# A scratch tile of 64 bytes a partition instead of 32, in front of the last SBUF pool

## The chip, the cores and the metric

The kernel runs on one core of one Trainium2 chip. The core has a matmul engine (TensorE, PE in the profile; its weight loads have a row of their own, PEld), a vector engine (VectorE, DVE), a scalar engine (ScalarE, ACT), GpSimd (POOL), and a queue engine (SyncE, SP) that here does nothing but issue transfers. Operands lie in SBUF, a memory of 128 partitions; an address here means the byte offset within a partition. Matmul results go to PSUM. The metric is device time in microseconds (us) of one execution. All sizes of SBUF tiles below are bytes a partition.

## The reference: what is computed

One encoder layer over 1024 positions of 1024 channels, in float32. A vector `c` gives six modulation rows through `silu(c) @ w_ada + b_ada`: shift, scale and gate (`gt1`, `gt2`) of two sub-layers.

```python
h = rmsnorm(x, norm1_g) * (1.0 + sc1) + sh1
u, v, q, k, va, gate_a, gate_b = split(h @ w_in)
a_out = gmlp_branch(u, v, ...) @ w_a
b_out = window_attention_branch(q, k, va, ...) @ w_b
merged = sigmoid(gate_a) * a_out + sigmoid(gate_b) * b_out
x = x + gt1 * (merged @ w_o)
h2 = rmsnorm(x, norm2_g) * (1.0 + sc2) + sh2
f_gate, f_up = split(h2 @ w_ffn_in)
x = x + gt2 * ((silu(f_gate) * f_up) @ w_ffn_out)
```

The attention looks at most 128 positions away and has 8 heads of 64; the feed-forward part (FFN) is 2816 wide.

## The kernel before, in words

**Split matmuls.** Each float32 operand is stored as a high part in the matmul's own number format (`fp32r`) and a low part that holds the rest. A product of two blocks is then three matmuls: high by high, high by low, low by high. ScalarE writes the high parts (`A.copy`), VectorE subtracts for the low parts. In the profile a matmul line names its PSUM bank first (`mm` or `at`) and then the two operands, in alphabetical order: `at<-tt1h,wh` has the weights `wh` as the stationary operand and the token tile `tt1h` as the moving one. All the big matmuls are 128 rows by 128 columns of weights against 512 moving columns.

**Stages.** `half(0)` and `half(1)` compute the normalised input, the input projections, the gMLP branch, the attention and the branch projections for the two halves of the positions. `gate_products` computes the sigmoid gates and the merge for six of the eight channel blocks, `out_products` the projection with `w_o` and the sums for the second norm. Then come the first and the second FFN matrix. From `gate_products` on, each 2 by 2 block product is done with seven block products instead of eight: sums of blocks are formed on VectorE first. The seven steps are listed in `STEPS` (line 1374), and each is 12 matmuls (`multiply`, line 1378). In their order, the moving operand is `B11`, `B21`, `T2`, `T1`, `T3`, `B22`, `T4`. `gate_products` runs the seven steps 6 times, the first FFN matrix 22 times (of its first six units the first two steps are done ahead), and `out_products` has them 4 times in another order.

**Where the moving operands lie.** `B11` and `B21` lie in `hpool` (tiles `h`), `T3` and `T4` in `mid`. `T1`, `T2` and `B22` lie in the pool `ffn` (tiles `tt1h`, `tt1l`, `tt2h`, `tt2l`, `b22h`, `b22l`, made by `fpt`, line 1248). The weights come from `wpool` (`wh`, `wl`), with one exception: the weights `first`, of two units, lie in `ffn`. In the second FFN matrix (`step_mm`) both operands of a step lie in one tile: 512 weight columns and 512 token columns side by side, for three steps of five in `wpool` (`wh`, `wl`), for the other two in the pool `outp` (`oh`, `ol`).

**The pools.** SBUF pools are laid one behind another in the order in which they are opened, and the tiles in a pool likewise; each tile's size is rounded up to a multiple of 32 bytes. The order is `const`, `wpool` (9 tiles of 4096), `hpool` (4 of 8192), `mid` (8 of 8192), `t2` (8 of 2048), `small`, and behind `small` one pool after another at the same place: `apool` with `attp` behind it during the two halves, then `ffn` from `open_ffn` on (line 573), then `outp` (line 2126). The tiles of `small`, rounded, with their numbers:

| tile of `small` | bytes, number | sum |
|---|---|---|
| `es`, `ms`, `qms`, `qrs`, `nmx`, `den`, `vr`, `ngt` | 32, 4 of each | 1024 |
| `ss` | 2560, 1 | 2560 |
| `kms`, `krs` | 64, 4 of each | 512 |
| `ngt1` | 32, 1 | 32 |
| all | | 4128 |

`wpool`, `hpool`, `mid` and `t2` are together 151552 bytes, a multiple of 2048. So the last pool begins 151552 + 4128 = 155680 bytes behind the start of `wpool`, and 155680 = 64 x 2432 + 32. The tiles of `ffn` and `outp` are all 4096 or 8192 bytes, and every matmul operand begins at a multiple of 512 within its tile. So an operand in `ffn` or `outp` and an operand in `wpool`, `hpool` or `mid` lie a multiple of 64 plus 32 bytes apart, and two operands of `wpool`, `hpool` and `mid` a multiple of 512 apart, as are two operands that both lie in `ffn` or `outp`. In `apool` the key tile `kbuf` too lies a multiple of 64 plus 32 bytes from `wpool`, and so do the tiles of `attp` (`pH`, `pL`, `vt`).

**The order of the work.** In `half` and `gate_products` the instructions of each engine run in the order of the program. In `out_products` a small planner (`Plan`) orders them by written costs; it knows nothing of addresses. The FFN's order is written out by hand (`tc.manual_schedule`).

Of the kernel before, what the change touches and what calls it, by code (L numbers as in the profile page):

```python
# [8 lines left out]
F32 = mybir.dt.float32  # L9
# [3 lines left out]
ALU = mybir.AluOpType  # L13
# [3 lines left out]
P = 128  # L17
D = 1024
S = 1024
KT = D // P  # L20
# [87 lines left out]
def kernel(  # L108
# [43 lines left out]
    V, A, G, T = (Engine(e) for e in (nc.vector, nc.scalar, nc.gpsimd, nc.tensor))  # L152
# [8 lines left out]
    small = ctx.enter_context(pool("small", 4))  # L161
# [21 lines left out]
    def midt(dt, shape):  # L183
        return mid.tile([P, 2048], dt, tag="mid", name=nm("mid")).rearrange(
            "p (a b) -> p a b", a=shape
        )
# [6 lines left out]
    def sm(n, name):  # L193
        return small.tile([P, n], F32, tag=name, name=nm(name))
# [76 lines left out]
    mod = const.tile([P, 48], F32, tag="mod", name="mod")  # L271
    acc_mod = const.tile([P, 48], F32, tag="acc_mod", name="acc_mod")
    SH1, SC1, GT1, SH2, SC2, GT2 = (8 * i for i in range(6))
# [1217 lines left out]
    def out_products(merged):  # L1491
# [5 lines left out]
        B22 = oblk["B22"] = (fpt("b22h"), fpt("b22l"))  # L1497
        T3 = oblk["T3"] = (midt(F32R, 4), midt(F32R, 4))
        T4 = oblk["T4"] = (midt(F32R, 4), midt(F32R, 4))
        ngt = small.tile([P, KT], F32, tag="ngt1", name="ngt1", bufs=1)  # L1500
        V.tensor_scalar(ngt, mod[:, GT1 : GT1 + KT], -1.0, None, op0=ALU.mult)
        gt = mod[:, GT1 : GT1 + KT]

        def negsum(out, a, b):
# [279 lines left out]
    with tc.manual_schedule():  # L1784
        out_products(merged)
# [263 lines left out]
    with tc.manual_schedule():  # L2049
# [141 lines left out]
        ngt = sm(4, "ngt")  # L2191
# [130 lines left out]
```

## Time and profile before

| what | us |
|---|---|
| median of 3 runs | 1232.06 |
| lowest, highest of the runs | 1232.01, 1233.99 |
| the profiled execution's own time | 1234.32 |
| its span, first to last instruction | 1232.5 |
| PE busy in the span | 1220.7 |
| DVE busy | 928.6 |
| ACT busy | 582.6 |
| granted TensorE clock, mean | 0.999 |

The profile is of one execution. Its span is the time from the first to the last instruction on the chip; the execution's own time stands 1.8 us above it. Matmuls overlap: one that is shown with 390 ns may begin 227 ns after the one before. What a matmul costs in a row of them is therefore the distance between starts. The chain view gives that: it follows the work that ended last back from the end and merges pieces of one kind, so that a piece `x12` of 2.72 us is twelve matmuls, one every 227 ns.

### The profile page before, as it was taken

To read this page: it belongs to the slowest core of one execution; us is meant where nothing else is said; L and a number is where in the kernel's file an instruction comes from. 1 tells how busy PE (TensorE), PEld (TensorE's weight loads), DVE (VectorE), ACT (ScalarE), POOL (GpSimd) and SP (SyncE) were. 2 spreads that over 40 slices of the span, in tenths; PEclk is the share of its full clock that TensorE was granted. 3 is DMA by queue.
4 is the path that set the end of the run, shared out by engine and by line. 5 is a ranking of instruction groups with operands and counts; after the bars stand their busy time and mean duration, and the time that the engine had idled before them with its cause. 6 is when DMAs were issued, how large, how long until landed. Compare 5 with 4: busy or idle time off the path is not lost.

```text
span 1232.5 us, 15626 instructions
## 1 busy us (share of the span) xinstructions
PE 1220.7 (99%) x5653; PEld 1006.7 (82%) x5653; DVE 928.6 (75%) x1504; ACT 582.6 (47%) x954; POOL 150.6 (12%) x182
## 2 busy tenths in 40 slices
PE   8999999999999999999999999999999999999998
PEld 7888888888788888878778888888888888888887
DVE  8999977789978766898897667575676766665646
ACT  5667855367855443645453333333333334433341
POOL 0024323114322000011000000000000000010001
PEclk9999999999999999999999999999999999999999
DMA  9752169654276333476403446454555439995552
GB/s 363 275 185 96 35 228 362 230 188 154 103 258 237 110 113 104 147 232 227 137 35 120 171 158 218 177 187 182 188 188 188 169 147 366 394 357 188 188 171 103
DMA packets 78096, 236.54 MB, mean 192 GB/s; under 512 B 8898, under 2 KB 9154, under 8 KB 72772
## 3 DMA queue, kind: packets, MB, share of 16 engines
q1 hardware_dynamic: 63028, 163.20, 38.4%
q0 software_dynamic: 14992, 72.36, 15.6%
q8 instruction: 44, 0.72, 0.2%
q14 instruction: 32, 0.26, 0.1%
HBM read 176.28 MB, written 59.24 MB: 191 GB/s over the span
## 4 chain that ended last, share of the span: by engine, by line
PE 91%; DVE 4%; DMA 2%; ACT 2%; issue 1%; SPq 0%; ACTq 0%; DVEq 0%
PE mm L145 46%; PE at L145 45%; DVE mid L145 2%; DMA raw<-in_w_q_dram 1%; DMA ws<-in_w_up_dram 1%; DVE wl L145 0%; ACT lb L145 0%; DMA mid<-in_xA_dram 0%; ACT mid L145 0%; DVE lb L145 0%; ACT pH L145 0%; DVE wo L145 0%; DVE ss L145 0%; DVE pL L145 0%; DVE xs L145 0%
## 5 line engine op out<-in xcount | busy, mean ns | idle before, releaser
L145 DVE TENSOR_TENSOR wl<-raw,wh 128x1024 fp32r<-128x1024 f32 (+1 forms) x135 | 158.8, 1180 | 61.7 <-ACT wh L145 61.2
L145 ACT CAST wh<-raw 128x1024 fp32r<-128x1024 f32 (+1 forms) x149 | 152.0, 1022 | 110.9 <-PE mm L145 36.4
L145 PE MATMUL mm<-mid,wh 128*128 128x512 f32 x640 | 198.7, 391 | 0.7 <-DVE mid L145 0.7
L145 PEld LDWEIGHTS mm<-mid,wh 128*128 128x128 f32 x640 | 119.8, 188 | 26.8 <-DVE mid L145 1.1
L145 PE MATMUL mm<-wh,h 128*128 128x512 f32 x384 | 124.6, 396 | 1.6 <-ACT h L145 1.6
L145 PE MATMUL mm<-mid,wl 128*128 128x512 f32 x320 | 124.9, 390 | 0.0
L145 PE MATMUL at<-h,wh 128*128 128x512 f32 x304 | 94.1, 391 | 1.3 <-DVE t L145 1.3
L145 PE MATMUL mm<-h,wh 128*128 128x512 f32 x304 | 94.3, 391 | 0.0
L145 PEld LDWEIGHTS mm<-wh,h 128*128 128x128 f32 x384 | 70.8, 188 | 15.2 <-ACT h L145 1.9
L145 DVE TENSOR_TENSOR wl<-ws,wh 128x1024 fp32r<-128x1024 f32 (+1 forms) x54 | 60.7, 1124 | 25.0 <-ACT wh L145 25.0
L145 ACT CAST wh<-ws 128x1024 fp32r<-128x1024 f32 (+1 forms) x54 | 52.6, 973 | 43.8 <-DVE ws L145 31.5
L145 PE MATMUL mm<-wl,h 128*128 128x512 f32 x192 | 71.2, 391 | 0.0
L145 PEld LDWEIGHTS mm<-mid,wl 128*128 128x128 f32 x320 | 60.0, 188 | 13.6
L145 PEld LDWEIGHTS at<-h,wh 128*128 128x128 f32 x304 | 56.8, 188 | 13.7 <-DVE t L145 2.1
L145 PEld LDWEIGHTS mm<-h,wh 128*128 128x128 f32 x304 | 56.6, 188 | 11.7
L145 ACT ACTIVATE t<-t 128x512 f32<-128x512 f32 x46 | 28.4, 630 | 71.7 <-DVE t L145 71.6
L145 DVE TENSOR_TENSOR ol<-raw,oh 128x1024 fp32r<-128x1024 f32 x30 | 36.6, 1223 | 31.4 <-ACT oh L145 29.8
L145 PE MATMUL mm<-h,wl 128*128 128x512 f32 x152 | 59.3, 390 | 0.0
L145 PE MATMUL at<-h,wl 128*128 128x512 f32 x152 | 59.2, 389 | 0.0
L145 ACT ACTIVATE xs<-xs 128x512 f32<-128x512 f32 x21 | 13.3, 632 | 96.2 <-DVE xs L145 96.2
L145 PE MATMUL at<-wl,wh 128*128 128x512 f32 (+1 forms) x136 | 52.8, 389 | 0.0
L145 PE MATMUL at<-wh 128*128 128x512 f32 (+1 forms) x136 | 52.8, 388 | 0.0
(296 smaller groups left out, 2866.0 us busy)
## 6 DMA issues: line engine op xcount, KB each, us to landing
mid<-in_w_ada_dram SPq DMA_DIRECT2D x28, 512.0 KB, 8.8
raw<-in_w_gate_dram SPq DMA_DIRECT2D x28, 512.0 KB, 3.8
tA<-hid POOLq DMA_DIRECT2D x11, 1024.0 KB, 4.4
tB<-hid POOLq DMA_DIRECT2D x11, 1024.0 KB, 5.0
wo<-in_w_out_dram POOLq DMA_DIRECT2D x22, 512.0 KB, 6.1
wS<-wo POOLq DMA_DIRECT2D x11, 1024.0 KB, 5.3
raw<-wS SPq DMA_DIRECT2D x44, 256.0 KB, 3.1
raw<-tB SPq DMA_DIRECT2D x44, 256.0 KB, 5.3
```

The lines of the kernel that those rows point to most:

```text
L145: ins = f(*args, **kw)
```

## The change

The tile `ngt1`, which holds the negated gates of the first sub-layer in `out_products`, is made 16 floats wide instead of 8. Only its first 8 columns are written and read. It takes 64 bytes instead of 32 in `small`, so `small` takes 4160 bytes instead of 4128. `ngt`, which stands behind `ngt1`, and everything in the pools behind `small` (`apool`, `attp`, `ffn`, `outp`) begin 32 bytes higher. The distance from `wpool` to the last pool becomes 155712 = 64 x 2433, an odd number of 64s. The pools before `small` stay where they are, and no instruction is added, removed or moved to another engine.

```diff
@@ -1497,8 +1497,8 @@
         B22 = oblk["B22"] = (fpt("b22h"), fpt("b22l"))
         T3 = oblk["T3"] = (midt(F32R, 4), midt(F32R, 4))
         T4 = oblk["T4"] = (midt(F32R, 4), midt(F32R, 4))
-        ngt = small.tile([P, KT], F32, tag="ngt1", name="ngt1", bufs=1)
-        V.tensor_scalar(ngt, mod[:, GT1 : GT1 + KT], -1.0, None, op0=ALU.mult)
+        ngt = small.tile([P, 16], F32, tag="ngt1", name="ngt1", bufs=1)
+        V.tensor_scalar(ngt[:, :KT], mod[:, GT1 : GT1 + KT], -1.0, None, op0=ALU.mult)
         gt = mod[:, GT1 : GT1 + KT]
```

## Prediction

> **What bounds the kernel now.** I read the page first: the busy times, the granted clock, the chain by engine.
>
> ```profile
> span 1232.5 us, 15626 instructions
> PE 1220.7 (99%) x5653; PEld 1006.7 (82%) x5653; DVE 928.6 (75%) x1504; ACT 582.6 (47%) x954; POOL 150.6 (12%) x182
> PEclk9999999999999999999999999999999999999999
> PE 91%; DVE 4%; DMA 2%; ACT 2%; issue 1%; SPq 0%; ACTq 0%; DVEq 0%
> ```
>
> TensorE is busy for 99% of the span at the full granted clock, and the chain that ends last runs through it for 91%. The reader is to see that the matmuls are the bound and that the clock isn't. So the question is whether a matmul itself can be cheaper. The chain view in order of time (start, length, what) shows that equal matmuls do not cost the same. The long run of 204 matmuls is from the end of the second half, the next rows are from the gate products, the others from the FFN:
>
> ```profile
> 346.97 46.28 PE mm L145 x204
> 412.61 2.72 PE at L145 x12
> 415.32 2.80 PE mm L145 x12
> 418.13 2.80 PE at L145 x12
> 420.93 2.76 PE mm L145 x12
> ...
> 763.41 5.48 PE mm L145 x24
> 768.89 2.72 PE at L145 x12
> 771.61 2.80 PE mm L145 x12
> 774.41 2.80 PE at L145 x12
> 777.21 2.76 PE mm L145 x12
> 779.97 2.80 PE at L145 x12
> 782.77 5.48 PE mm L145 x24
> ```
>
> Read from 768.89: the seven steps of one FFN unit, twelve matmuls each, in the order of the code. B21 takes 2.72, T2 2.80, T1 2.80, T3 2.76, B22 2.80, and the last piece of 24 is T4 with the next unit's B11, 5.48. From 763.41 to 782.77 is one period: 19.36 us for 84 matmuls. In the long run of 204 one matmul takes 46.28 / 204 = 226.9 ns, in a step of 2.72 it takes 226.7 ns, in one of 2.80 it takes 233.3 ns. All three steps of 2.80 have their moving operand in the pool `ffn`; no other step has. T3, with its operand in `mid`, follows such a step and takes 2.76.
>
> Who is slow is told by operand in the groups kept apart by form. The means are modelled durations, longer than the distance between starts, but they differ by the same 5 to 6 ns:
>
> ```profile
> L145 PE MATMUL mm<-mid,wh 128*128 128x512 f32 x640 | 198.7, 391 | 0.7 <-DVE mid L145 0.7
> L145 PE MATMUL at<-h,wh 128*128 128x512 f32 x304 | 94.1, 391 | 1.3 <-DVE t L145 1.3
> L145 PE MATMUL at<-tt1h,wh 128*128 128x512 f32 x112 | 44.3, 395 | 0.0
> L145 PE MATMUL at<-tt2h,wh 128*128 128x512 f32 x88 | 34.9, 396 | 0.0
> L145 PE MATMUL mm<-b22h,wh 128*128 128x512 f32 x72 | 28.6, 397 | 0.0
> L145 PE MATMUL at<-oh,ol 128*128 128x512 f32 x84 | 32.9, 391 | 0.0
> L145 PE MATMUL at<-pH,vt 128*128 128x512 f32 x44 | 17.4, 396 | 0.0
> L145 PE MATMUL mm<-h,first 128*128 128x512 f32 x24 | 5.9, 395 | 0.0
> ```
>
> Now put the distances between the two operands beside them, taken to multiples of 64 bytes. `mid` or `h` with `wh`: no remainder, 391. `tt1h`, `tt2h`, `b22h` with `wh`: 32 bytes over, 395 to 397. `first` with `h`: here the weights lie in `ffn` and the moving operand doesn't, 32 over again, 395. `oh` with `ol`: both in the last pool, no remainder between them, 391. So it is not the pool's place that costs, nor an operand that begins off a multiple of 64 by itself. It is a pair whose two operands lie 32 bytes apart in that count. One row speaks against it: `pH` with `vt`, both in `attp`, is slow at 396 without a remainder. Those come in runs of two to six between shapes of another kind, and T3 above shows that a pair without remainder needs a run-in: its first twelve take 2.76 and not 2.72. I take the row for such a run-in.
>
> **The change part by part.** The instruction that writes the wider tile is the same one, over the same 8 columns (172 ns, below), and it stays where the planner put it: 0. Everything behind `small` moves by 32 bytes. What else works on those tiles is not sensitive to the place:
>
> ```profile
> L145 DVE TENSOR_SCALAR ngt<-mod 128x8 f32<-128x8 f32 x1 | 0.2, 172 | 0.0
> L145 DVE TENSOR_TENSOR tt1l<-mid,tt1h 128x512 fp32r<-128x512 f32 x12 | 8.0, 684 | 1.4 <-ACT tt1h L145 1.4
> L145 DVE TENSOR_TENSOR mid<-mid,mid 128x512 fp32r<-128x512 f32 x26 | 16.9, 683 | 0.1
> L145 ACT CAST tt1h<-mid 128x512 fp32r<-128x512 f32 x12 | 7.2, 618 | 6.2 <-DVE mid L145 6.1
> L145 ACT CAST mid<-mid 128x512 fp32r<-128x512 f32 x26 | 14.8, 620 | 6.5 <-DVE mid L145 6.4
> ws<-in_w_up_dram SPq DMA_DIRECT2D x11, 512.0 KB, 5.7
> ru<-in_w_up_dram SPq DMA_DIRECT2D x11, 512.0 KB, 3.6
> ```
>
> VectorE takes 684 ns with `ffn` and 683 without, ScalarE 618 and 620. The same weights land in 3.6 us in `ru`, which is in `ffn`, and in 5.7 us in `ws`, which is in `mid`: 32 bytes cost a transfer nothing that shows. All these terms are 0, covered by a TensorE that is busy 99% in any case.
>
> The matmuls, for pairs that after the change lie an odd number of 64s apart:
> - Steady. Three steps in the `ffn` pool, 12 matmuls each, in 6 + 22 units of the gates and the FFN and 4 of `out_products`: 32 x 36 = 1152 matmuls. 233.3 - 226.7 = 6.6 ns each: 7.6 us.
> - Run-ins. T3 and T4 follow such a step in each of 28 units: 2.76 - 2.72 = 0.04 us, 56 times: 2.2 us. In `out_products` two or three more: 0.1.
> - The 48 matmuls with `first` save 0.3 us by the same price, but they end in the stretch below where VectorE is late: 0. That stretch is what comes next when a matmul gets cheaper: from 593.56 to 621.55 the chain leaves TensorE, waits for a transfer and then goes through VectorE. It starts from sums that follow the matmuls before it, so what is won before it is kept, and what is won inside it is not.
>
> ```profile
> 593.56 6.64 DMA ws<-in_w_up_dram
> 600.22 0.70 DVE ws L145
> 621.55 30.86 PE at L145 x132
> ...
> 1017.85 60.11 PE at L145 x264
> ```
>
> - The second FFN matrix. 60.11 / 264 = 227.7 ns against 226.7: the run-ins between `wh` and `oh`, 1.0 ns x 924 matmuls = 0.9 us. A pair of it that straddles the switch goes from 32 over to none, so it may gain all of it or none; I take 0.4.
> - The attention. `kbuf` comes level with its weights, but in runs of two matmuls, which stay in the run-in: 0, at most 0.5.
>
> Sum: 7.6 + 2.2 + 0.1 + 0.4 = 10.3 us. TensorE must find its operands that much earlier. In the FFN this is no difficulty:
>
> ```profile
> 800.00:900.00 100.00, 100.00 (x436) 81.36 (x435) 67.51 (x94) 33.16 (x46) 7.60 (x15) 1.00 0.50 179
> 900.00:1000.00 100.00, 100.00 (x436) 81.44 (x435) 67.96 (x95) 34.10 (x47) 9.60 (x18) 1.00 0.54 191
> ```
>
> In these rows of 100 us (PE, PEld, DVE, ACT, POOL busy, then clock and DMA share) VectorE has 32 us to spare and the DMA engines half their time; 1.6% more speed leaves that cover standing. I take off 0.3 for waits elsewhere: 10.0 us. Against the profiled span, 1232.5 to 1222.5; its own time of 1234.32 is the launch's 1.8 us more and lies 2.3 above the median shown, which is where the next forecast starts: 1232.06 - 10 = 1222.
>
> The unknown in this: the trace of before has no row of a pair 64 bytes over. All its pairs are a multiple of 512 apart or 32 over. Both ends come from the nearest rows. If 64 over is like none, -10.3. If the cost grows with the distance, 32 bytes are 6.6 ns and 64 are 13.2: the same terms again with the other sign, +10. I take the first, because the rows come back to the same 391 for two quite different no-remainder cases (`mid` with `wh`, and `oh` with `ol`), and a pattern that repeats every 64 bytes is the shortest that fits them.
>
> [...]
>
> **The rivals.**
> - *64 over is a worse phase, not a good one.* The place is the same 1152 matmuls. For it: no pair in the trace has this distance, and a pattern that repeats every 128 bytes fits the rows too. Against it: it would have to lie beyond the 233.3 that 32 over gives, and no steady row is slower than that. It decides once the new steady step takes more than 2.80. Price: 1152 x 6.6 ns = 7.6, run-ins another 2.2: 1242.
> - *The shift does nothing to the pairs.* Either the cost is that of the tiles' high place in SBUF, or it repeats in a way in which 64 over costs what 32 over does, or the place doesn't matter at all and the steps differ for another reason. [...] For it: `ffn` and `attp` are both high and both slow. Against it: `oh` and `ol` lie at the same height and are fast, and `first` makes a slow pair with a fast `h`. Time: 1232.
> - *The matmuls get cheaper and the gain is only half kept.* The run-ins stay (they follow any switch) or other waits take it: 7.6 us less some 2: 1226. For it: the gates have VectorE nearer its limit than the FFN. Against it: the chain of the FFN is TensorE alone.
>
> **How the numbers follow.** The forecast, 64 over like none, 0.68, with its own range 1219.5 to 1225; half kept, 0.09 (1225 to 1229); nothing, 0.08 (1229.6 to 1234.5); worse phase, 0.15 (1235 to 1244). A measurement of this kernel can tell about 0.2%, or 2.5 us, from no change. So faster 0.77, the same 0.08, slower 0.15. The range 1219.5 to 1233 leaves out the worse phase and some 0.04 at the edges.
>
> **What would show it.** Right: the three `ffn` steps of an FFN unit take 2.72 instead of 2.80 in the chain, T3 and T4 too, the period goes from 19.36 to 19.04, and the groups with `tt1h`, `tt2h`, `b22h` come down from 395 to 397 to about 391; the group of `oh` stays. The DVE and ACT rows above stay. Wrong: the three steps stay at 2.80 (the pairs don't matter) or go past it (worse phase); or they fall and the span doesn't, and then a wait ahead of PE on DVE or a transfer shows where it went.

## The result, and the profile after

The changed kernel takes 1229.3 us (median of 7 runs, 1227.43 to 1231.04) beside 1233.99 us of the kernel before (7 runs, those shown above among them): a ratio of 0.9964 with a 95% interval of 0.9951 to 0.9976. By that ratio it is 4.4 us faster (3.0 to 6.0); the medians differ by 4.7. The forecast was 10 us, and the gain lies between the likeliest case and no change. The forecast of 1222 us was also counted from a median of three runs, 1232.06; with seven runs the median of the kernel before is 1.9 us higher.

The page of the changed kernel, the lines that answer to those of before:

```profile
span 1229.2 us, 15626 instructions
PE 1217.7 (99%) x5653; PEld 1007.4 (82%) x5653; DVE 928.8 (76%) x1504; ACT 582.5 (47%) x954; POOL 150.8 (12%) x182
```

The span is 3.3 us shorter, and PE's busy time fell by 3.0: what was won came out of the matmuls, as it should, since the busy time of the other engines stayed. The chain of the changed kernel in order of time (start, length, what), the end of the second half first, then one FFN unit from B21 to T4 with the next B11, then a piece of the second FFN matrix:

```profile
347.22 46.27 PE mm L145 x204
...
761.68 5.49 PE mm L145 x24
767.17 2.72 PE at L145 x12
769.89 2.76 PE mm L145 x12
772.65 2.75 PE at L145 x12
775.40 2.77 PE mm L145 x12
778.17 2.76 PE at L145 x12
780.93 5.49 PE mm L145 x24
...
1014.74 60.05 PE at L145 x264
```

T2, T1 and B22 take 2.76, 2.75, 2.76 where they took 2.80. T3 behind them takes 2.77 where it took 2.76, and T4 with B11 5.49 instead of 5.48: the run-ins are still there. The period is 780.93 - 761.68 = 19.25 us, against 19.36 before and 19.04 forecast. The groups by operand say the same. In these rows the moving operand stands first and the weights second, not in the order of the alphabet: the page has both `at<-oh,ol` and `at<-ol,oh`. Two rows of the kernel before, beside the one with `tt1h,wh` above:

```profile
L145 PE MATMUL at<-tt1h,wl 128*128 128x512 f32 x112 | 44.2, 395 | 0.0
L145 PE MATMUL at<-tt1l,wh 128*128 128x512 f32 x112 | 44.2, 395 | 0.0
```

And the changed kernel:

```profile
L145 PE MATMUL at<-tt1h,wh 128*128 128x512 f32 x112 | 44.2, 395 | 0.0
L145 PE MATMUL at<-tt1h,wl 128*128 128x512 f32 x112 | 43.9, 392 | 0.0
L145 PE MATMUL at<-tt1l,wh 128*128 128x512 f32 x112 | 43.5, 388 | 0.0
L145 PE MATMUL at<-oh,ol 128*128 128x512 f32 x84 | 32.8, 391 | 0.0
L145 PE MATMUL at<-pH,vt 128*128 128x512 f32 x44 | 17.2, 390 | 0.0
L145 DVE TENSOR_TENSOR tt1l<-mid,tt1h 128x512 fp32r<-128x512 f32 x12 | 8.1, 685 | 1.4 <-ACT tt1h L145 1.4
L145 ACT CAST tt1h<-mid 128x512 fp32r<-128x512 f32 x12 | 7.2, 618 | 6.8 <-DVE mid L145 6.7
```

Of the three matmuls of a group, all at 395 before, one is now at 388, one at 392 and one still at 395. These are modelled durations, and the steps of the chain are the surer measure: 2.75 to 2.76 us, between 2.72 and 2.80. VectorE and ScalarE work on the moved tiles as fast as ever (685 and 618 ns).

So the steps do change with the distance, and the question for the runs was which distances are good, and whether it is the distance that counts or the place of one tile by itself. Below, a pair or a kernel is called level when the distance is a multiple of 256 bytes, and "over" is the distance between the last pool and `wpool` less the nearest lower multiple of 256 bytes: 32 before, 64 in the changed kernel. The level kernel is the one of the first run.

### The profile page after: what moved, and what is told of

Same layout as the page of the kernel before. It is cut to its first block, busy times and chain, and to the rows that moved or that the text cites. A ratio compares the mean times of both kernels' runs of the same rounds, so it can differ in the third digit from the quotient of the medians.

```text
span 1229.2 us, 15626 instructions
## 1 busy us (share of the span) xinstructions
PE 1217.7 (99%) x5653; PEld 1007.4 (82%) x5653; DVE 928.8 (76%) x1504; ACT 582.5 (47%) x954; POOL 150.8 (12%) x182
## 4 chain that ended last, share of the span: by engine, by line
PE 92%; DVE 4%; DMA 2%; ACT 1%; issue 1%; SPq 0%; DVEq 0%; ACTq 0%
PE at L145 47%; PE mm L145 46%; DVE mid L145 1%; DMA raw<-in_w_q_dram 1%; DMA raw<-in_w_ada_dram 1%; DVE wl L145 1%; DVE t L145 0%; DMA mid<-in_xA_dram 0%; DVE wo L145 0%; DVE raw L145 0%; DVE pL L145 0%; ACT wh L145 0%; ACT mid L145 0%; DVE ss L145 0%; DVE tt1l L145 0%
## 5 line engine op out<-in xcount | busy, mean ns | idle before, releaser
L145 ACT CAST oh<-raw 128x1024 fp32r<-128x1024 f32 x30 | 31.6, 1054 | 45.3 <-PE at L145 23.6
```

Source lines behind the costliest of these rows:

```text
L145: ins = f(*args, **kw)
```

## The experiments

The times of the first four kernels are to be compared with 1233.56 us for the kernel before (median of 11 runs), those of the next four with 1235.43 and that of the last with 1233.02 (one run each). Only the first of these kernels ran more than once; for the others the steps in the trace carry the argument, not the single time.

**No remainder at all.** The negated gates use a buffer that `small` has anyway, so that the last pool begins 32 bytes lower than before.

```diff
-        ngt = small.tile([P, KT], F32, tag="ngt1", name="ngt1", bufs=1)
+        ngt = sm(NH, "qms")
```

> The negated gates use a buffer of another tag of 32 bytes, so that the last pool begins 32 bytes lower than before, 155648 = 2048 x 76 bytes behind wpool; nothing else differs. Theory 1 (the distance between the two operands of a pair sets the cost, and it repeats only after more than 64 bytes): the steps in the ffn pool take 2.72 us, the run-ins of T3 and T4 go too (2.72 instead of 2.77), the FFN period is 19.04 us and the time some 10 us under before, 1222 to 1224. Theory 2 (what costs is the start of a tile off a multiple of 64 by itself, and the changed kernel already has all of that gain): the same as the changed kernel, steps of 2.76, 1229.

Measured: 1223.96 us (median of 6 runs, 1220.86 to 1225.04), ratio to before 0.9919, 95% interval 0.9905 to 0.9932. That is 10.0 us less (8.4 to 11.7). The chain of this kernel, one FFN unit:

```profile
758.56 5.44 PE mm L145 x24
...
764.00 2.72 PE at L145 x12
766.72 2.72 PE mm L145 x12
769.44 2.72 PE at L145 x12
772.16 2.72 PE mm L145 x12
774.88 2.72 PE at L145 x12
777.60 5.44 PE mm L145 x24
...
1008.80 59.84 PE at L145 x264
```

Every step takes 2.72, T3 and T4 too, and the period is 777.60 - 758.56 = 19.04. Theory 1 holds, theory 2 falls: this pool starts on a multiple of 64 as that of the changed kernel does, and is some 5 us faster. Its tiles lie as high in SBUF as before but for 32 bytes, so the height doesn't cost anything either.

**128 over, and 256.** The scratch tile is made wider.

```diff
-        ngt = small.tile([P, 16], F32, tag="ngt1", name="ngt1", bufs=1)
+        ngt = small.tile([P, 32], F32, tag="ngt1", name="ngt1", bufs=1)   # 128 over
+        ngt = small.tile([P, 64], F32, tag="ngt1", name="ngt1", bufs=1)   # 256
```

> The scratch tile takes 128 bytes, the last pool begins 155776 bytes behind wpool, 128 over a multiple of 256. Theory 1 with a period of 128 bytes: steps of 2.72 and 1222 to 1224. Theory 1 with a longer period: steady steps of another length, between 2.72 and 2.80 or outside. Theory 2: 2.76 and 1229.

> The scratch tile takes 256 bytes, the last pool begins 256 over a multiple of 512 behind wpool. Theory 1 with a period of 128 or 256 bytes: steps of 2.72, 1222 to 1224. With a period of 512 or more: another length. Theory 2: 2.76 and 1229.

Measured: 1229.28 with 128 over, 1224.04 with 256. The chain with 128 over, from T2 to B22:

```profile
768.14 2.79 PE mm L145 x12
770.93 2.80 PE at L145 x12
773.73 2.73 PE mm L145 x12
776.47 2.79 PE at L145 x12
```

And with 256, T2 and T3:

```profile
766.46 2.72 PE mm L145 x12
...
771.90 2.72 PE mm L145 x12
```

At 128 the `ffn` steps are nearly as slow as at 32 and the run-ins almost gone (2.73), so that the single time is that of 64 over; at 256 all is as with no remainder. The 2.72 comes back at 256 and not at 64 (2.75 to 2.76) or 128 (2.79 to 2.80).

**Moving the others instead.** An unused pool of 32 bytes behind `wpool`.

```diff
+    gap = ctx.enter_context(pool("gap")).tile([P, 8], F32, tag="gap", name="gap")
     hpool = ctx.enter_context(pool("hpool", 4))
```

> An unused pool of 32 bytes between wpool and hpool: hpool, mid and t2 now lie 32 over from wpool, the ffn pool 64 over as in the changed kernel. Theory 1: the slow steps change places: B11, B21, T3 and T4 take 2.80, the ffn steps 2.76, the FFN period is about 4 x 2.80 + 3 x 2.76 = 19.5 us, and the two halves, whose moving operands lie in hpool and mid, get slower too: about 2500 matmuls with 5 to 6.6 ns, 12 to 16 us, less the 4 of the ffn pool, so 1240 to 1245. A theory that the tiles' high place in SBUF is what costs: the steps in h and mid stay at 2.72 and the time at 1228 to 1232.

Measured: 1238.9 us, 5.3 over before and 1.1 under the expected range. The chain, first the long run of 204 at the end of the second half, then T4 with B11, B21, T2, T1, T3:

```profile
349.65 47.60 PE mm L145 x204
...
767.27 5.59 PE mm L145 x24
772.86 2.80 PE at L145 x12
775.66 2.75 PE mm L145 x12
778.41 2.75 PE at L145 x12
781.16 2.79 PE mm L145 x12
```

The slow steps have changed places: the operands in `hpool` and `mid`, fast in every other kernel so far, now take 2.79 to 2.80, and those in `ffn`, 64 over, 2.75. New about these tiles are their distance from the weights and, with it, their own start; the next run keeps the two apart. The size falls short of the expectation, and it does so in the two halves. The long run pays the full price, 47.60 - 46.28 = 1.32 us or 6.5 ns a matmul. But at its end this kernel is only 4.0 us behind the kernel before (397.25 against 393.25), where 12 to 16 had been expected. Why the matmuls ahead of it lost so little, no run shows.

**Moving all of them.** The same 32 bytes ahead of `wpool`.

```diff
+    gap = ctx.enter_context(pool("gap")).tile([P, 8], F32, tag="gap", name="gap")
     wpool = ctx.enter_context(pool("wpool", 3))
```

> An unused pool of 32 bytes ahead of wpool: every big tile lies 32 bytes higher than before the change and all distances between pools are those of before. Theory 1 (the distance of a pair counts, taken to multiples of 256 bytes): all as before, steps of 2.72, 2.80, 2.80, 2.76, 2.80, period 19.36, 1232 to 1235. Theory 3 (the moving tile's own start counts, off multiples of 64 it is slow): the steps in hpool and mid, now 32 off, go to 2.80 and the ffn steps, now on a multiple of 64, fall to about 2.75: 1240 to 1245.

Measured: 1234.84 us, beside 1235.43. From T4 with B11 on:

```profile
763.90 5.48 PE mm L145 x24
769.38 2.72 PE at L145 x12
772.10 2.80 PE mm L145 x12
774.90 2.80 PE at L145 x12
777.70 2.76 PE mm L145 x12
```

To the hundredth the steps of before, though every start has moved. It is the distance, not the start of either operand. Theory 3 falls.

**192 and 96 over.** The scratch tile of 192 and of 96 bytes (`[P, 48]` and `[P, 24]`).

> The scratch tile takes 192 bytes, the last pool begins 192 over a multiple of 256 behind wpool, and its tiles begin at multiples of 256 of the partition. Theory 1: not the fast step, since the distance is no multiple of 256: between 2.75 and 2.80, run-ins at T3 and T4, 1227 to 1233. Theory 3 in the form that a start on a multiple of 256 is fast: steps of 2.72 and about 1223.

> The scratch tile takes 96 bytes, distance 96 over a multiple of 256. Theory 1: between 2.75 (64 over) and 2.80 (128 over), or the same 2.80 as 32 over if every odd 32 is equally bad; 1228 to 1233. Theory 3: off multiples of 64 again, 2.80 and 1232.

Measured: 1231.61 and 1231.96. T2 and T3 with 192 over, then T2, T1 and T3 with 96:

```profile
769.56 2.80 PE mm L145 x12
...
775.15 2.74 PE mm L145 x12
```

```profile
768.41 2.81 PE mm L145 x12
771.22 2.80 PE at L145 x12
774.02 2.76 PE mm L145 x12
```

With 192 over, the tiles of `ffn` start on multiples of 256 of the partition, and they are slow all the same: theory 3 is out in that form too.

**16 over, for T1 alone.** On the level kernel, with the T1 tiles longer and used from their 16th byte on.

```diff
+        if name in ("tt1h", "tt1l"):
+            t = fps[0].tile([P, 2048 + 64], F32R, tag=name, name=nm(name))
+            return t[:, 4 : 4 + 2048].rearrange("p (a b) -> p a b", a=4)
```

> The last pool as in the kernel with the gates in the other tag (all distances multiples of 256), but the T1 tiles are 256 bytes longer and used from their 16th byte on, so that T1 alone lies 16 over. Theory 1: the T1 step leaves 2.72, between 2.72 and 2.80, the step T3 behind it shows a run-in, T2 and B22 stay at 2.72; a T1 step under 2.72 would mean that a multiple of 256 isn't the best distance. If only whole lines of 32 bytes count: T1 stays at 2.72.

Measured: 1225.81 us. T1, T3, B22:

```profile
769.86 2.78 PE at L145 x12
772.64 2.75 PE mm L145 x12
775.38 2.72 PE at L145 x12
```

T1 costs 0.06 more, T3 behind it 0.03, the others nothing (T2, ahead of T1, takes 2.72 too). Even 16 bytes count: 2.78 here against 2.72 in the level kernel.

**Only the low weights off.** Everything level, but the `wl` tiles 32 bytes longer and used from their 32nd byte on; a gap pool of 160 bytes behind `wpool` makes the rest level again.

```diff
+    def low_tile():
+        return wpool.tile([P, UNIT + 8], F32R, tag="wl", name=nm("wl"))[:, 8:]
...
-        l = wpool.tile([P, UNIT], F32R, tag="wl", name=nm("wl"))
+        l = low_tile()
```

> The last pool and hpool, mid and t2 all lie multiples of 256 behind wpool; only the low weight tiles wl are moved, by 32 bytes in each of three buffers that are 4128 apart, so they lie 32, 64 and 96 over from everything else (in the attention's own weight tiles 0, 32 and 64). In each group of three matmuls (wh with the high token tile, wh with the low, wl with the high) the weights of the third are then off. Theory 1a (the pair of one and the same matmul counts): the third, at<-tt1h,wl, rises from 389 to 392 to 396, at<-tt1l,wh ahead of it stays at 389. Theory 1b (what counts is the weights of the next matmul, which are loaded while the one before still streams): the second, at<-tt1l,wh, rises to 392 to 396 and the third stays at 389 but for run-in. In both the time goes up from the level kernel by 1 to 1.5 ns over all matmuls, 1228 to 1236.

Measured: 1243.25 us, some 19 over the level kernel and well outside what was expected. The groups of this kernel:

```profile
L145 PE MATMUL at<-tt1l,wh 128*128 128x512 f32 x112 | 44.3, 396 | 0.0
L145 PE MATMUL at<-tt1h,wh 128*128 128x512 f32 x112 | 44.2, 395 | 0.0
L145 PE MATMUL at<-tt1h,wl 128*128 128x512 f32 x112 | 44.0, 393 | 0.0
L145 PE MATMUL at<-oh,ol 128*128 128x512 f32 x84 | 32.9, 391 | 0.0
```

All three matmuls of a group are slow (389 to 390 in the level kernel), the one whose own pair is off least of all (393), the one ahead of it most (396). That leans to the loading of the next weights (theory 1b), but neither theory had expected the first of the group, `at<-tt1h,wh`, to rise. What this kernel shows is that one pair in three off is enough to keep every matmul slow. That fits the run-in of T3 in the kernel before, in which seven intervals in a row are disturbed (224 to 241 ns): here only two level ones lie between. `oh` with `ol`, which have no `wl`, take 391 as in the kernel before (389 in the level kernel).

The trace of the kernel before can tell the two theories apart. In the second FFN matrix both operands of every matmul lie in one pool, so no matmul has an own pair that is off. Only at a switch does a tile stream from one pool while the weights of the next matmul are loaded from the other, 32 over. The first switch from `wpool` to `outp` in the kernel before (PEld is the weight load):

```profile
1025.62 0.40 PE L145 MATMUL at<-wh,wl 128*128 128x512 f32 x1
1025.62 0.19 PEld L145 LDWEIGHTS at<-oh 128*128 128x128 f32 x1
1025.86 0.39 PE L145 MATMUL at<-oh 128*128 128x512 f32 x1
```

The weights from `oh` load while the tile in `wpool` streams, and the next matmul starts 235 ns behind, by the trace's starts before they are rounded. So it does at all 30 switches, those back to `wpool` included. In the level kernel the same 30 take 226 or 227, and a run of 264 with switches in it averages 59.84 / 264 = 226.7. In the changed kernel, 64 over, they take 225 or 226, so there the switch itself costs nothing. An own pair that is off can't be the reason here. What counts at these switches, as far as they show it, is the moving tile and the weights loaded beside it for the next matmul, theory 1b. In the steps of the gates and the first FFN matrix all these weights lie in `wpool`, except `first`, so there the two theories give the same and the runs above hold for either.

## Why the prediction was right in kind and wrong in size

Point by point, by its own steps.

- *TensorE bounds the kernel and the clock does not.* Right. PE was busy for 99% of the span before and after, and the granted clock was 0.998 to 1.000 in all the runs. In the level kernel the sum of 10.3, less 0.3 for waits, came out as 10.0, so nearly all of what matmuls save reaches the time.
- *The cost belongs to a pair whose operands lie 32 bytes apart.* Right as to the distance: the two shifted kernels move the slow steps to other tiles, or move everything and leave them. Not quite right as to the pair: at the switches of the second FFN matrix it is the moving tile and the weights of the next matmul, the pair that the prediction called straddling (235 ns at 32 over, 226 or 227 level).
- *VectorE, ScalarE and the transfers are not sensitive to the place.* Right: 685 and 618 ns against 684 and 618, and `ru` in `ffn` lands in 3.5 us against 3.6.
- *The unknown: "If 64 over is like none, -10.3."* This is the step that failed. The prediction took that end because a pattern that repeats every 64 bytes was the shortest that fitted. But both of its no-remainder cases lie a multiple of 512 apart, so they fit a period of 64, 128, 256 or 512 alike and could not choose. The 2.72 came back only at multiples of 256: of the remainders tried, 0, 32, 64, 96, 128 and 192 for the last pool and 16 for T1 alone, only 0 gives 2.72, and 64 gives 2.75 to 2.76.
- *The steady term, 7.6 us.* Right sign, too large. T2, T1 and B22 fell by 0.04, 0.05 and 0.04 instead of 0.08 each, 0.13 us for a group of three steps, times 32 groups: 4.2 us.
- *The run-ins, 2.2 us.* Wrong. They did not go, since `ffn` and `mid` are still not level with each other: 2.77 instead of 2.76, 5.49 instead of 5.48, 0.01 us the other way, 56 times: 0.6 us lost. Nor do the "first twelve" share a run-in evenly: by the trace's starts, T3 behind T1 has seven intervals of 224 to 241 ns and then five of 226 or 227 in the kernel before, and ten disturbed ones in the changed kernel. The half-kept rival had the run-ins staying, but it kept the steady term whole and took some 2 off for run-ins or waits; that its 1225 to 1229 ends next to the measured 1229.3 is in part luck.
- *The second FFN matrix, 0.4 us.* 60.11 - 60.05 = 0.06 us for 264 matmuls, 0.2 for 924. Its run-ins stay for the same reason; in the level kernel they are gone (59.84, which makes 0.9 for 924, all of what the prediction halved to 0.4).
- *The attention, 0 to 0.5.* `pH` with `vt` fell from 396 to 390, but no gain of it shows in the time: the two halves end at 393.49 instead of 393.25, 0.2 us later.

Together 4.2 - 0.6 + 0.2 - 0.2 = 3.6 us: the profiled span lost 3.3, the medians differ by 4.7. The rival on the slow side was wrong in sign for 64: of all the remainders tried other than 0, its steady steps cost least. And the forecast sum was not far off as a sum: it is about what a distance of a multiple of 256 brings, and that kernel, at 1223.96, beats both the changed kernel and the one before. The kernel with a scratch tile of 256 bytes, one run at 1224.04, does the same with the edit that this case made, only wider.

What stays open is why. The distance alone changed the step from 2.72 to 2.80 us and, at the switches, the interval from 226 or 227 to 235 ns; how it does so, no run told.

## What to carry to other kernels

In a kernel that TensorE bounds, look at whether equal matmuls take equal time in the chain; where they don't, compare the SBUF addresses of the moving tiles and the weights before anything else. For the 128x512 `fp32r` matmuls of this kernel, a distance of a multiple of 256 bytes between every two pools of operands was worth 0.8% (1223.96 us against 1233.56), and 64 over less than half of that (a ratio of 0.9964). A remainder that no row of the trace shows has to be priced as unknown between its ends, and the shortest pattern that fits is not yet the likely one.

## What the runs showed of the hardware that was not expected

- In these kernels the time of a row of matmuls changed with the distance between the moving tile and the weights, taken to multiples of 256 bytes. At the switches of the second FFN matrix, where every matmul's own pair is level, it went with the weights loaded for the next matmul: 235 ns at 32 over, 225 or 226 at 64 over, 226 or 227 level. Twelve matmuls took 2.72 us at 0 and at 256, 2.78 at 16, 2.80 at 32, 2.75 to 2.76 at 64, 2.80 to 2.81 at 96, 2.79 to 2.80 at 128 and 2.80 at 192.
- The slowdown carries over. Twelve level matmuls behind a step that was off took between 2.73 (behind 128) and 2.77 (behind 64) instead of 2.72, and with one weight tile in three off all three matmuls of a group were slow (393 to 396 ns against 389 to 390), for 19 us in all.
